# A head's normalised rows are transposed by DMAs in 16-bit planes instead of by TensorE

## The chip, the cores and the metric

The kernel runs on one core of one Trainium2 chip. The metric is the device time of one execution in microseconds (us). Before the change it is 894.45 us (median of 3 runs, 894.21 to 894.65). The engines that matter here are TensorE (PE in the profile, with PEld for its weight loads), VectorE (DVE), ScalarE (ACT), GpSimd (POOL) and SyncE (SP), which issues the DMAs.

## What is computed

One layer of a hybrid decoder: 16 learned meta tokens are put ahead of 2048 rows of 1024 features, the rows are normalised and multiplied by one input projection of eight groups of 512 columns, four groups feed a gated short convolution, four feed a retention layer of four heads, and the two results are joined, multiplied by an output projection, added to the input and normalised again. All is float32.

```
proj = rms_norm(h, norm_g) @ w_in                       # 2064 x 4096
cx, cb, cc, cg, q, k, v, rg = split(proj, 8)
conv_out = short_conv(cx, cb, cc) * silu(cg)
ret = head_group_norm(retention_chunkwise(rotary(q) * d**-0.5, rotary(k), v), ret_norm_g)
ret_out = ret * silu(rg)
y = rms_norm(h + concat(conv_out, ret_out) @ w_out, final_g)[16:]

def head_group_norm(o, g):                              # over the 128 features of a head
    y = (o - mean(o)) * rsqrt(var(o) + 1e-6)
    return y.reshape(rows, 512) * g
```

## The kernel before

The 2048 rows are taken in two blocks of 1024 (`r` = 0, 1), each as two halves of 512 rows (`j` = 0, 1). The projection is computed transposed: features lie on the 128 partitions and rows run along the free dimension, because a matmul there has a weight block as its stationary operand and 512 rows as its moving one. Each block runs through eight **units**: `UNITS` (line 37) gives their order. Units 0 to 3 are the heads of the retention, units 4 to 7 the groups of the convolution. After both blocks the output projection takes eight pairs of 128-row tiles.

A unit makes its projections in two **quads** (`quad`, line 203): seven products in the manner of Strassen and Winograd for a 2x2 arrangement of blocks, each product 12 matmuls of 128x512 (line 212), since every operand is split into a high and a low part and three of their four combinations are used. ACT casts the high part `wh` of a weight block (line 101), DVE subtracts it to get the low part `wl` (`sub`, line 113), from a ring of three buffers each, so that a cast waits until PE has finished the product three places back. Three of a quad's products are copied out of their PSUM bank by ACT (`copy`, line 219, tile `tc`, called here a bank copy), the second of them because PE then adds to the same bank. The results go to `take`, which adds, rotates or gates them on DVE and ACT.

A head (`head`, line 575) takes k and v from its first quad, q and the gate `sg` from its second. Then follow, for each half, transposes of k and v on PE (lines 631, 636), the state updates (646, 649), the scores (659, masked on DVE into the tile `pm`, line 661), the output `o` (669, 670), and the group norm: statistics on DVE (675, 677), a power on POOL (682), and four 128x128 operations on DVE that write the normalised rows `y` over `pm` (686). At that point rows lie on the partitions and features along the free dimension, while `sg` and all that follows has features on the partitions. So four PE matmuls against `ident` (line 693) transpose the four chunks of 128 rows into the PSUM tile `yT`, one DVE operation (694) multiplies `yT` by the norm's gain and by `sg`, and `store_mixed` (line 441, its DMA at 444) sends the half to DRAM in `mixed`, from which the output projection reads it. `pm` and `kd` (line 633) share two buffers (tag `b`), and so a head's `kd` waits until the `pm` of the head before is free.

The row tiles (`row_tile`, line 341) are 128x1024 float32 tiles in four buffers: the two rows of norm factors of each block, scratch at the start, loads for the output projection near the end, and `final_g`.

The program is recorded in this order, but its place on each engine is chosen by a scheduler, which moves an instruction ahead where its own timing says that another would wait; so the tail of a head stands among the matmuls of the next unit's quads. Each engine then runs its list in order, and SP too: a DMA that waits for its data holds up those behind it. Between heads SP also loads the raw weights of the following quads (`ra`, line 436) and eight tiles `x` or `w` (lines 361, 368), of which DVE makes sums that are stored for later (`prepare`, lines 181 to 191).

## Time and profile before

| | us |
|---|---|
| median of 3 runs | 894.45 |
| the profiled execution, its own time | 893.76 |
| the span of its instructions | 892.0 |
| of that, ACT busy | 407.2 |
| of that, POOL busy | 397.8 |

The profiled execution is 0.69 us below the median and just below the lowest run. The span begins with the first instruction and ends with the last, and 1.76 us of the execution's own time lie around it. The stretches of the span: the first block's units from about 57 to 365 us (heads to about 258, whose tail runs to 303), the second block's from 365 to 709 (heads to about 553, tails to 607), the output projection from 709 on.

How to read the rows: a timeline row has the start, the time from start to end, the engine, the line of the kernel, the operation, the tiles it writes and reads with their shape, a count, and in brackets how long the engine had been idle and who released it. PE's matmuls are pipelined: each overlaps the next, so the time from one start to the next is what a matmul takes of the engine, and its duration is longer. Each matmul of the lines 646, 659, 669 and 670, on plain float32 operands, appears as two records; those of line 212 and the transposes as one.

### The profile page before, as it was taken

What the parts mean: (1) busy time and instruction counts of PE and PEld (TensorE: products, weight loads), DVE (VectorE), ACT (ScalarE), POOL (GpSimd) and SP (SyncE); (2) the same over time, 40 slices, a digit from 0 to 9 for tenths busy, and PEclk for the clock granted to TensorE, in tenths of its full rate; (3) what the DMA queues carried; (4) which work ended last, traced back from release to release, by engine and by line L of the source; (5) the groups of instructions that cost most, each with busy time, mean ns of one, the idle gap of its engine ahead of it and who ended that gap; (6) DMA issues with size and microseconds to landing.
All of it is one profiled execution on the core that took longest, in us unless ns stands there. A gap on an engine that the chain in (4) does not pass through costs nothing.

```text
span 892.0 us, 12867 instructions
## 1 busy us (share of the span) xinstructions
PE 879.8 (99%) x4407; PEld 725.0 (81%) x4407; DVE 717.7 (80%) x1176; ACT 407.2 (46%) x816; POOL 397.8 (45%) x291
## 2 busy tenths in 40 slices
PE   8999999999999999999999999999999999999996
PEld 5778788888888778888888888888888888788885
DVE  6788887988967966999889899777668699766764
ACT  8674424234245364746243332423333476545553
POOL 0554222313134654452323323345546454787773
PEclk9999999999999999999999999999999999999999
DMA  9711224354224252834135272313131393555532
GB/s 336 231 65 48 72 54 150 129 159 149 73 83 142 83 154 75 293 117 141 48 95 200 71 245 87 96 58 95 49 93 49 117 390 101 183 165 160 183 121 81
DMA packets 76242, 116.94 MB, mean 131 GB/s; under 512 B 7632, under 2 KB 24336, under 8 KB 76176
## 3 DMA queue, kind: packets, MB, share of 16 engines
q1 hardware_dynamic: 76176, 116.11, 40.3%
q8 instruction: 35, 0.57, 0.3%
q14 instruction: 31, 0.25, 0.1%
HBM read 90.92 MB, written 25.17 MB: 130 GB/s over the span
## 4 chain that ended last, share of the span: by engine, by line
PE 82%; DVE 8%; DMA 4%; issue 2%; ACT 2%; POOL 2%; SPq 0%; POOLq 0%; DVEq 0%; ACTq 0%
PE pj L212 66%; PE pj L262 6%; DVE ml L113 2%; PE ms L669 1%; PE ms L670 1%; PE ms L659 1%; PE ms L646 1%; DMA w<-in_w_out 1%; DMA ra<-in_w_in 1%; PE ms L397 1%; DVE wl L113 1%; PE ms L693 1%; DVE ml L105 1%; PE ms L631 1%; PE ms L636 1%
## 5 line engine op out<-in xcount | busy, mean ns | idle before, releaser
L212 PE MATMUL pj<-mh,wl 128*128 128x512 f32 x1008 | 399.1, 396 | 1.5 <-ACT wh L101 0.6
L212 PE MATMUL pj<-ml,wh 128*128 128x512 f32 x1008 | 393.3, 390 | 0.0
L212 PE MATMUL pj<-mh,wh 128*128 128x512 f32 x1008 | 393.0, 390 | 0.0
L101 ACT CAST wh<-ra 128x512 fp32r<-128x512 f32 x216 | 134.0, 621 | 311.0 <-PE pj L212 264.9
L212 PEld LDWEIGHTS pj<-mh,wl 128*128 128x128 f32 x1008 | 189.4, 188 | 43.2 <-issue 2.2
L113 DVE TENSOR_TENSOR wl<-ra,wh 128x512 fp32r<-128x512 f32 x216 | 194.1, 899 | 34.5 <-ACT wh L101 34.0
L212 PEld LDWEIGHTS pj<-mh,wh 128*128 128x128 f32 x1008 | 189.2, 188 | 39.9
L212 PEld LDWEIGHTS pj<-ml,wh 128*128 128x128 f32 x1008 | 189.5, 188 | 37.8 <-issue 0.5
L113 POOL TENSOR_TENSOR ra<-ra 128x512 f32<-128x512 f32 x72 | 112.8, 1566 | 84.1 <-DVE qg L614 32.3
L110 POOL TENSOR_TENSOR sa<-ra 128x512 f32<-128x512 f32 x36 | 54.9, 1526 | 120.6 <-DVE wl L113 53.1
L113 POOL TENSOR_TENSOR ra<-sa,ra 128x512 f32<-128x512 f32 x36 | 52.0, 1444 | 92.6 <-DVE wl L113 89.1
L219 ACT COPY tc<-pj 128x512 f32<-128x512 f32 x108 | 62.7, 580 | 0.0
L262 PE MATMUL pj<-ml,mh 128*128 128x512 f32 x128 | 50.2, 392 | 0.1
L262 PE MATMUL pj<-mh,mh 128*128 128x512 f32 x128 | 49.9, 392 | 0.0
L262 PE MATMUL pj<-mh,ml 128*128 128x512 f32 x128 | 48.7, 397 | 0.7 <-DVE ml L113 0.6
L682 POOL TENSOR_TENSOR rp<-rs,neg_half 128x4 f32<-128x4 f32 x16 | 19.9, 1246 | 48.1 <-DVE rs L110 47.8
L723 DVE TENSOR_TENSOR yo<-pj,yo 128x512 f32<-128x512 f32 x32 | 21.9, 686 | 17.6 <-PE pj L212 7.8
L101 ACT CAST wh<-sa 128x512 fp32r<-128x512 f32 x36 | 22.4, 621 | 29.1 <-PE pj L212 28.9
L522 POOL TENSOR_TENSOR c<-c,rr 128x512 f32<-128x512 f32 x14 | 26.1, 1865 | 19.6 <-DVE c L459 9.6
L686 DVE TENSOR_SCALAR pm<-ms,mv,rp 128x128 f32<-128x128 f32 x64 | 21.9, 404 | 15.8 <-POOL rp L682 15.8
L522 POOL TENSOR_TENSOR c<-c,tc 128x512 f32<-128x512 f32 x14 | 26.1, 1862 | 18.7 <-ACT tc L548 18.7
L728 POOL TENSOR_TENSOR z<-yo,final_g 128x512 f32<-128x512 f32 x16 | 26.9, 1682 | 15.9 <-DVE yo L723 15.9
(137 smaller groups left out, 1145.5 us busy)
## 6 DMA issues: line engine op xcount, KB each, us to landing
ra<-in_w_in SPq DMA_DIRECT2D x128, 256.0 KB, 2.7
x<-in_xT SPq DMA_DIRECT2D x48, 256.0 KB, 4.8
w<-in_w_out SPq DMA_DIRECT2D x32, 256.0 KB, 5.2
ra<-mixed SPq DMA_DIRECT2D x32, 256.0 KB, 2.6
yo<-in_x SPq DMA_DIRECT2D x32, 256.0 KB, 4.5
ra<-in_x SPq DMA_DIRECT2D x16, 256.0 KB, 3.2
mixed<-c SPq DMA_DIRECT2D x16, 256.0 KB, 2.6
mixed<-qg SPq DMA_DIRECT2D x16, 256.0 KB, 2.3
```

Source lines behind the costliest of these rows:

```text
L101: nc.scalar.copy(out=hi, in_=src)
L105: nc.vector.scalar_tensor_tensor(out=lo, in0=src, scalar=scale, in1=hi.bitcast(F32), op0=ALU.mult, op1=ALU.subtract)
L110: eng.tensor_tensor(out=out, in0=a, in1=b, op=ALU.add)
L113: eng.tensor_tensor(out=out, in0=a, in1=b, op=ALU.subtract)
L212: nc.tensor.matmul(bank, a[:, ks], b, start=first and kt == 0 and n == 0, stop=kt == KH - 1 and n == 2, skip_group_check=not first,)
L219: nc.scalar.copy(out=c, in_=bank)
L262: nc.tensor.matmul(banks[i], a[:, ks], b, start=half + kt + n == 0, stop=half == 1 and kt == KH - 1 and n == 2,)
L522: eng.tensor_tensor(out=out, in0=a, in1=b, op=ALU.mult)
L682: nc.gpsimd.tensor_tensor(out=rp, in0=rs, in1=neg_half.rearrange("p (c a) -> p c a", a=1), op=ALU.pow)
L686: nc.vector.tensor_scalar(out=y[:, cs], in0=o[:, cs], scalar1=mv[:, c, 0:1], scalar2=rp[:, c, :], op0=ALU.subtract, op1=ALU.mult,)
L723: last[0] = nc.vector.tensor_tensor(out=y, in0=pp, in1=y, op=ALU.add)
L728: nc.gpsimd.tensor_tensor(out=ys[i][j], in0=y, in1=final_g[:, j * HB : (j + 1) * HB], op=ALU.mult)
```

## The change

PE's four transposes for each half, the PSUM tile `yT` and the DVE operation that read it go. In their place each half is transposed by one DMA:

- ACT copies `y` into a row tile `apart`, seen as 16-bit words: all low halves of the float32 words first, then all high halves (two planes of 512 words; line 716 after the change).
- SP issues a transposing DMA from `apart` to a second row tile `across`, eight blocks of 128x128 16-bit words (line 717).
- ACT puts the planes of `across` together again into float32 words, in `apart` (722). DVE multiplies by gain and gate as before, now from `apart` in SBUF (723), and `store_mixed` follows.

The first two steps (`turn`) are recorded within the next unit, after its first quad, and the last (`finish`) after its second quad. `catch_up` records them under `issue_after` the last bank copy of that quad, so that on ACT they stand behind the quad's bank copies. The two row tiles are those of the other block's pair (`rr0` or `rr1`, two buffers each instead of four in common), which hold nothing at that time.

```diff
     def quad(w, m, take):
         def copy(bank):
             c = sb.tile([P, HB], F32, name="tc", tag="tc", bufs=COPIES)
-            nc.scalar.copy(out=c, in_=bank)
+            copied[0] = nc.scalar.copy(out=c, in_=bank)
             return c
...
-    def row_tile(name):
-        return sb.tile([P, BLK], F32, name=name, tag="rr", bufs=4)
+    def row_tile(name, pair):
+        return sb.tile([P, BLK], F32, name=name, tag=f"rr{pair}", bufs=2)
...
+    def halves(a):
+        return a.bitcast(U16).rearrange("p (n two) -> p two n", two=2)
+
+    def planes(a):
+        return a.bitcast(U16).rearrange("p (two n) -> p two n", two=2)
+
+    waiting = [[], []]
+
+    def catch_up(stage):
+        if waiting[stage]:
+            with tc.issue_after(copied[0].ins):
+                while waiting[stage]:
+                    waiting[stage].pop(0)()
...
             quad(stationary(blocks[0]), m, take)
+            catch_up(0)
...
             quad(stationary(load_raw(w_loads(2 * h + 1))), m, take)
+            catch_up(1)
...
-            yT = ps_misc()
-            for c in range(CH):
-                cs = slice(c * P, (c + 1) * P)
-                nc.tensor.transpose(yT[:, cs], y[:, cs], ident)
-            nc.vector.scalar_tensor_tensor(
-                out=sg[j], in0=yT, scalar=ret_g[:, h : h + 1], in1=sg[j], op0=ALU.mult, op1=ALU.mult
-            )
-            store_mixed(r, j, KH + h, sg[j])
+            def turn(j=j, y=y, apart=turning[0][:, j * HB : (j + 1) * HB], across=turning[1][:, j * HB : (j + 1) * HB]):
+                nc.scalar.copy(out=planes(apart), in_=halves(y))
+                nc.sync.dma_start(
+                    across.bitcast(U16).rearrange("p (c f) -> p c f", c=2 * CH), apart.bitcast(U16), transpose=True
+                )
+
+                def finish():
+                    nc.scalar.copy(out=halves(apart), in_=planes(across))
+                    nc.vector.scalar_tensor_tensor(
+                        out=sg[j], in0=apart, scalar=ret_g[:, h : h + 1], in1=sg[j], op0=ALU.mult, op1=ALU.mult
+                    )
+                    store_mixed(r, j, KH + h, sg[j])
+
+                waiting[1].append(finish)
+
+            waiting[0].append(turn)
...
+                if turning is None:
+                    turning = [row_tile(name, 1 - r) for name in ("apart", "across")]
```

The convolution groups call `catch_up` in the same two places. Three places show how the lists of the engines move; all are of the first block, where the tail of head 1 runs beside the quads of head 2. Numbers behind a name tell one buffer from another and differ between the two programs.

On PE, in head 2's first quad before the change, the transposes of half 0 (line 693) stand with the scores of half 1 (659):

```order
L212 MATMUL pj_1935<-mh02_139,wl_1904 128x512
L212 MATMUL pj_1935<-ml02_140,wh_1903 128x512
L212 MATMUL pj_1935<-mh02_139,wh_1903 128x512
L693 MATMUL ms_1667<-ident_70,pm_1638 128x128
L659 MATMUL ms_1674<-qg_1512,kv_1358 128x128
L693 MATMUL ms_1667<-ident_70,pm_1638 128x128 x3
L659 MATMUL ms_1674<-qg_1512,kv_1358 128x128 x3
L212 MATMUL pj_1935<-mh03_145,wl_1904 128x512
```

After the change the scores of half 1 (now line 682) follow at once on the last output matmuls of half 0 (now lines 692 and 693, which were 669 and 670):

```order
L692 MATMUL ms_1638<-kv_1365,pm_1636 128x128
L693 MATMUL ms_1638<-state_1598,qg_1440 128x128
L682 MATMUL ms_1665<-qg_1504,kv_1346 128x128 x4
L215 MATMUL pj_1816<-mh50_234,wl_1760 128x512
L215 MATMUL pj_1816<-ml50_235,wh_1759 128x512
L215 MATMUL pj_1816<-mh50_234,wh_1759 128x512
```

The scores of half 1 move ahead by 33 of the 128x512 matmuls (before, 33 lie between the outputs of half 0 and the scores of half 1). The output of half 1 came 15 such matmuls behind its scores, and comes 24 behind them now.

On ACT, in head 2's second quad before the change, there are casts and bank copies (219), ahead of the gate (615):

```order
L585 COPY kv_1892<-pj_1783 128x512
L101 CAST wh_1915<-ra_1894 128x512
L101 CAST wh_1919<-sa_1902 128x512
L219 COPY tc_1948<-pj_1935 128x512
L101 CAST wh_1923<-ra_1898 128x512
L101 CAST wh_1927<-ra_1896 128x512
L219 COPY tc_1982<-pj_1935 128x512
L101 CAST wh_1931<-ra_1900 128x512
L219 COPY tc_1997<-pj_1984 128x512
L101 CAST wh_2266<-ra_2060 128x512
L615 ACTIVATE qg_2011<-qg_2011 128x512
```

The same stretch after the change, with one row more at its head:

```order
L716 COPY apart_729<-pm_1636 128x1024
L606 COPY kv_1876<-pj_1767 128x512
L102 CAST wh_1903<-ra_1882 128x512
L102 CAST wh_1907<-sa_1890 128x512
L222 COPY tc_1936<-pj_1923 128x512
L102 CAST wh_1911<-ra_1886 128x512
L716 COPY apart_729<-pm_1670 128x1024
L102 CAST wh_1915<-ra_1884 128x512
L222 COPY tc_1970<-pj_1923 128x512
L102 CAST wh_1919<-ra_1888 128x512
L222 COPY tc_1985<-pj_1972 128x512
L722 COPY apart_729<-across_730 128x2x512 x2
```

The copies into planes (716) come one ahead of the last `kv` copy and one among the second quad's casts, ahead of two of its three bank copies. Both copies back (722) come behind the third bank copy, ahead of the cast for the next unit's first product (101 before, 102 now) and of the gate.

On SP, at the same place before the change, the two stores of `mixed` (444) have weight loads between them, and the eight loads of `x` (361) stand behind the second store:

```order
L436 DMA ra<-in_w_in 128x512 x3
L444 DMA mixed_88<-qg 128x4x128
L436 DMA ra<-in_w_in 128x512 x2
L415 DMA mr<-in_rot_m 16x256
L436 DMA ra<-in_w_in 128x512
L444 DMA mixed_89<-qg 128x4x128
L361 DMA x<-in_xT 128x512 x8
```

After the change:

```order
L439 DMA ra<-in_w_in 128x512 x2
L717 DMA_TRANSPOSE across<-apart 128x8x128
L439 DMA ra<-in_w_in 128x512 x2
L717 DMA_TRANSPOSE across<-apart 128x8x128
L439 DMA ra<-in_w_in 128x512
L418 DMA mr<-in_rot_m 16x256
L439 DMA ra<-in_w_in 128x512
L447 DMA mixed_88<-qg 128x4x128
L447 DMA mixed_89<-qg 128x4x128
L364 DMA x<-in_xT 128x512 x8
```

A transposing DMA stands about where the first store stood and one among the weight loads behind it; both stores now stand together ahead of the `x` loads.

More of the change, by code (lines that the diff above doesn't have):

```diff
@@ L11 @@
 BF16 = mybir.dt.bfloat16
+U16 = mybir.dt.uint16
 AF = mybir.ActivationFunctionType
@@ L201, in prepared @@
                 parts(m, SUMS[n], kt, a)
+    copied = [None]
     def quad(w, m, take):
@@ L339, in spread_factors @@
         return rc2, ev
-    def row_tile(name):
-        return sb.tile([P, BLK], F32, name=name, tag="rr", bufs=4)
+    def row_tile(name, pair):
+        return sb.tile([P, BLK], F32, name=name, tag=f"rr{pair}", bufs=2)
     def row_factors(r, f):
-        f.extend([row_tile("rr"), row_tile("rr2"), []])
+        f.extend([row_tile("rr", r), row_tile("rr2", r), []])
         for j in range(2):
@@ L573, in rotary, with head @@
         turned[0] = nc.vector.tensor_tensor(out=a, in0=a, in1=rot[:, :w], op=ALU.add)
-    def head(h, r, m, rot_t, f, blocks, ahead, first=(), between=()):
+    def halves(a):
[8 more added lines that the diff above has]
+                    waiting[stage].pop(0)()
+    def head(h, r, m, rot_t, f, turning, blocks, ahead, first=(), between=()):
         between = iter(between)
@@ L597, in head @@
             quad(stationary(blocks[0]), m, take)
+            catch_up(0)
         next(between, lambda: None)()
@@ L621, in head @@
             quad(stationary(load_raw(w_loads(2 * h + 1))), m, take)
+            catch_up(1)
         next(between, lambda: None)()
@@ L805, in hybrid_trunk @@
             nc.sync.dma_start(cols, t["cols"])
-            t3 = [a[:, i * HB : (i + 1) * HB] for a in (row_tile("t3") for _ in range(2)) for i in range(2)]
+            t3 = [a[:, i * HB : (i + 1) * HB] for a in (row_tile("t3", 1) for _ in range(2)) for i in range(2)]
             t1 = [brief("t1") if n < BRIEF else sb.tile([P, HB], F32, name="t1", tag="tc", bufs=COPIES) for n in range(KH)]
@@ L835, in hybrid_trunk @@
         units = UNITS[r]
+        turning = None
         special = (first, between)
@@ L843, in hybrid_trunk @@
             elif unit < NG:
-                blocks = head(unit, r, m, rot_t, f, blocks, rest, *(special if unit == 0 else ()))
+                if turning is None:
+                    turning = [row_tile(name, 1 - r) for name in ("apart", "across")]
+                blocks = head(unit, r, m, rot_t, f, turning, blocks, rest, *(special if unit == 0 else ()))
                 if unit > 0:
@@ L850, in hybrid_trunk @@
                     idle = sb.tile([P, 2, BLK], F32, name="held", tag="rot_t", bufs=1)
-                    areas = [idle[:, 0], idle[:, 1], row_tile("held"), row_tile("held")]
+                    areas = [idle[:, 0], idle[:, 1], row_tile("held", 0), row_tile("held", 0)]
                     for i, a in enumerate(areas):
@@ L861, in hybrid_trunk @@
     m, b = moving(load_w_out)
-    final_g = row_tile("final_g")
+    final_g = row_tile("final_g", 1)
     nc.sync.dma_start(final_g, t["final_g"].partition_broadcast(P))
```

## The prediction

> **What bounds the kernel now.** I read the page's busy times first, then PE's waits, then busy time by stretch (each row: the stretch, its length, busy us of PE, PEld, DVE, ACT, POOL with record counts, granted clock, DMA share, GB/s).
>
> ```profile
> PE 879.8 (99%) x4407; PEld 725.0 (81%) x4407; DVE 717.7 (80%) x1176; ACT 407.2 (46%) x816; POOL 397.8 (45%) x291
> ...
> PE pj L212 <- ACT wh L101: 0.6, 1, 0.6
> ...
> PE ms L693 <- DVE pm L686: 0.3, 1, 0.3
> ...
> 107.00:303.00 196.00, 196.00 (x1126) 163.59 (x1125) 164.37 (x338) 74.90 (x163) 65.75 (x52) 1.00 0.36 115
> 414.00:553.00 139.00, 138.68 (x734) 118.19 (x734) 123.77 (x230) 47.29 (x92) 42.99 (x28) 1.00 0.39 124
> 553.00:709.00 156.00, 156.00 (x735) 130.59 (x734) 114.27 (x172) 56.11 (x100) 75.59 (x57) 1.00 0.25 75
> ```
>
> PE is the bound, at a granted clock of 1.00. Beside the heads' tails (first and second row) it is never idle for more than 0.3 us in all, and its longest waits there are tenths. DVE is next: 164 of 196 us and 124 of 139. So an instruction taken from PE shortens the span by its slot, as long as the others keep their distance.
>
> **What a transpose costs PE.** The group of all 64 transposes, and one group of four that stands alone among 128x512 matmuls, with eight score records of another head from the chain:
>
> ```profile
> L693 PE MATMUL ms<-ident,pm 128*128 128x128 f32 x64 | 12.2, 274 | 0.3 <-DVE pm L686 0.3
> ...
> 140.26 0.39 PE L212 MATMUL pj<-ml,wh 128*128 128x512 f32 x1
> 140.48 0.39 PE L212 MATMUL pj<-mh,wh 128*128 128x512 f32 x1
> 140.72 0.60 PE L693 MATMUL ms<-ident,pm 128*128 128x128 f32 x4
> 141.07 0.48 PE L212 MATMUL pj<-mh,wl 128*128 128x512 f32 x1
> 141.38 0.40 PE L212 MATMUL pj<-ml,wh 128*128 128x512 f32 x1
> ...
> 112.76 0.89 PE ms L659 x8
> ```
>
> The 274 ns of a record are latency; the slot is what counts. From 140.48 to 141.38 are 0.90 us, and two 128x512 matmuls take 2 x 0.227 of it, so four transposes cost 0.446 us, the switch back included. The chain's row agrees: eight small records in 0.89 us, 0.111 each. There are 8 heads x 2 halves = 16 such groups: 16 x 0.445 = **7.1 us**. The scores that stood with half of them stay, now merged with the output group.
>
> A rule of the Trainium skill weighs differently: "TensorE: Matmul & The Clock Gate", section "Part 4: PE-mode transpose", gives about 275 ns for a transpose in one kernel's context. The record's 274 ns agree with it, the 0.111 us slots do not; by 275 ns each, 64 would free 17.6 us.
>
> **The rest of the change, where it must hide.** ACT gets 16 copies into planes and 16 back, of 1024 words each. No ACT copy here is so long; nearest are these two groups and, from the second quad of head 2, the place where the copies will stand:
>
> ```profile
> L219 ACT COPY tc<-pj 128x512 f32<-128x512 f32 x108 | 62.7, 580 | 0.0
> ...
> L403 ACT COPY mk<-ms 16x128 f32<-16x128 f32 x32 | 8.1, 254 | 2.0 <-PE ms L397 1.6
> ...
> 185.89 0.62 ACT L101 CAST wh<-ra 128x512 fp32r<-128x512 f32 x1 [3.94 <-PE pj L212]
> 186.42 0.58 ACT L219 COPY tc<-pj 128x512 f32<-128x512 f32 x1
> 188.57 0.62 ACT L101 CAST wh<-ra 128x512 fp32r<-128x512 f32 x1 [1.57 <-PE pj L212]
> 189.10 0.58 ACT L219 COPY tc<-pj 128x512 f32<-128x512 f32 x1
> 191.29 0.62 ACT L101 CAST wh<-ra 128x512 fp32r<-128x512 f32 x1 [1.62 <-PE pj L212]
> ```
>
> 580 ns for 512 and 254 for 128 make 0.85 ns a word, so 1.02 us for 1024; if strides of two words cost double it is 2.0. I take 1.0: 32 us more on ACT, 407 to 440 of 892. ACT waits 1.6 to 3.9 us for PE between casts, which covers a copy; two in a row (line 722, 2.04 us) begin at 189.68 and push the cast of 191.29 to 191.7.
>
> When is the data there? The rows of half 1 set it, in the tail that runs beside head 2:
>
> ```profile
> 168.59 0.39 PE L670 MATMUL ms<-state,qg 128*128 128x128 f32 x2
> ...
> 181.13 0.38 PE L669 MATMUL ms<-kv,pm 128*128 128x128 f32 x2
> ...
> 188.54 1.37 DVE L686 TENSOR_SCALAR pm<-ms,mv,rp 128x128 f32<-128x128 f32 x4 [0.91 <-POOL rp L682]
> ...
> 191.96 0.74 DVE L694 SCALAR_TENSOR_TENSOR qg<-ms,ret_g,qg 128x512 f32<-128x512 f32 x1
> ...
> mixed<-qg SPq DMA_DIRECT2D x16, 256.0 KB, 2.3
> sums_w<-w SPq DMA_DIRECT2D x16, 256.0 KB, 2.0
> ...
> q1 hardware_dynamic: 76176, 116.11, 40.3%
> ```
>
> Half 0's output ends at 168.98. Now scores (0.89) and 24 matmuls (5.45) follow, so half 1's output starts at 175.3 instead of 181.13. `y` was whole at 189.91, 8.8 us after that start; with the same lag it is whole at 184.1. ACT, waiting for it since the cast at 181.33, copies until 185.1, ahead of the 185.89 cast.
>
> No transposing DMA is in the trace. Below, I bound issue to landing by the quickest transfer of its size, 2.0 us. Above: its output has pieces of 128 words of 16 bits, 1024 pieces, 64 for each of 16 engines; queue q1's packets take 0.403 x 892 x 16 / 76176 = 0.075 us on average, so 64 of them 4.8 us, and with 2.0 for the rest 6.8. I take 3, near the store of `mixed`, whose packets are the shortest of the large transfers. In a sentence by itself: the Trainium skill, "DMA: Bandwidth & Descriptors", section "Latency and other measured facts", has 261 GB/s for a DMA transpose, an estimate of 1.0 us for the 256 KB without the fixed part. So half 1 lands at 188, between 187.1 and 191.9; ACT comes to it at 189.7. On SP the transposes hold up weight loads behind them by at most these few us, and those serve products after 200.
>
> What is late next, if it slips? Behind ACT's copies back stand the cast of 191.29 and, through DVE and SP's second store, the `x` loads:
>
> ```profile
> 192.62 0.68 DVE L113 TENSOR_TENSOR wl<-ra,wh 128x512 fp32r<-128x512 f32 x1
> ...
> 204.22 0.68 DVE L113 TENSOR_TENSOR wl<-ra,wh 128x512 fp32r<-128x512 f32 x1
> ...
> 199.95 0.48 PE L212 MATMUL pj<-mh,wl 128*128 128x512 f32 x1
> ...
> 207.20 0.48 PE L212 MATMUL pj<-mh,wl 128*128 128x512 f32 x1
> ...
> 192.73 0.38 SPq L444 DMA_DIRECT2D mixed<-qg  x1
> 193.16 3.84 SPq L361 DMA_DIRECT2D x<-in_xT  x8
> ```
>
> The cast's low part is ready at 193.30 for a product at 199.95: 6.65 us of room. DVE's 723, of the 694's length, ends at 192.5 when the landing is in time, and the store goes out at about 192.7, as before. At the upper bound the copies back start at 191.9, and store and loads go out 2.0 us later; the sums of `x` then push the low part of 204.90, whose product starts at 207.20, and 2.3 us of room are there. Even the bound is covered, by 0.3 us. DVE's own work is the same in count and length (16 x 744 ns before, from PSUM).
>
> The second block is tighter. DVE at head 2's first quad there, and PE behind it:
>
> ```profile
> 489.16 0.65 DVE L113 TENSOR_TENSOR wl<-ra,wh 128x512 fp32r<-128x512 f32 x1
> ...
> 489.54 0.39 PE L212 MATMUL pj<-mh,wh 128*128 128x512 f32 x1
> 489.96 0.47 PE L212 MATMUL pj<-mh,wl 128*128 128x512 f32 x1
> ```
>
> PE waited 0.2 us here, since DVE had worked without a pause. In the new order DVE masks half 1's scores (0.74 us) ahead of this low part, but PE also gets half 1's output matmuls (about 1.7 us of slots) ahead of it, so I take nothing for the place, with bounds of -0.3 and +1.0 us for each of the three heads whose tail meets such a stretch.
>
> **The sum.** 892.0 - 7.1 = 884.9 us of span, with the 1.76 around it 886.7, against 893.76 for the profiled execution. That lies 0.69 below the median, so against the median the same sum is 894.45 - 7.1 = **887.4**. The bounds of the tight place move it from 886.5 to 890.4.
>
> **The rivals.** *Part given back* (0.13): ACT's in-order wait for `y`, or DVE's order in the second block, makes PE wait 0.5 us or more in most heads. For it: the 0.2 us wait above; against it: rooms of 2 to 6 us elsewhere. 2 to 4.5 us come back: 889.4 to 891.9. *Slower* (0.06): the transposing DMA lands later than assumed. From about 7.1 us to landing the 2.3 us of room at 207.20 are gone (half 1 leaves at 185.1, 189.7 is free, 192 is not), and each further us is one for PE in each of 8 heads. The gain is used up 0.9 us later, at 8.0; at 9 us it is 887.4 + 8 x 1.9 = 902.6. The trace's largest transfers of this size (5.2 us for `w`, on a loaded queue) speak against it, the missing row for it. *No effect* (0.07): DVE, at 84 to 89% beside the heads, becomes the bound, and PE waits for what it saves: 893 to 895. Against it: DVE still pauses for POOL and ACT there. *The whole record is freed* (0.02): PE's slots in the trace speak against it, but if a transpose blocked PE for its 274 ns, 17.5 us would go: 876.9. The page named above is on this side.
>
> **How the numbers follow.** The forecast has 0.70, and 0.02 is left for other gains. The range, 885.8 to 891.0, holds it and most of the first rival; below and above it lie less than two in ten. A difference of 0.2% (1.8 us) is about what a measurement of this kernel tells from none: faster means below 892.7. That is the forecast, the first and the last rival and the rest, 0.87; within it 0.07; slower 0.06.
>
> **What would show it.** Right: no PE record of 128x128 from `ident` and `pm`; PE idle by stretch still under 1 us beside the heads; landings of `across` at 2 to 5 us; the copies 716 and 722 at about 1.0 us; low parts of weights ahead of their products by 1 us or more. Wrong: PE waiting for ACT's casts or bank copies beside 716 and 722, landings over 7 us, copies over 2 us, or `x` and `w` loads that go out later against PE than before.

## The result, and the profile after

The changed kernel takes 886.98 us at the median (885.97 to 887.5, 4 runs), the kernel before 894.33 us beside it (893.01 to 894.65, 4 runs). The ratio is 0.9919, with an interval from 0.9902 to 0.9936. Forecast were 887.4 us, and 884.9 us of span.

The page of the changed kernel, its first line and the busy time of each engine:

```profile
span 884.9 us, 12802 instructions
...
PE 872.3 (99%) x4343; PEld 717.7 (81%) x4343; DVE 718.4 (81%) x1176; ACT 441.1 (50%) x848; POOL 400.4 (45%) x291
```

The span is 7.1 us shorter, PE's busy time 7.5 us (879.8 before). ACT has 34 us more, DVE is unchanged. What PE waits for in the changed kernel (us in all, times, longest):

```profile
PE ms L799 <- ACT warm L793: 2.3, 1, 2.3
PE pj L215 <- ACT tc L222: 1.0, 2, 0.6
PE pj L215 <- DVE wl L114: 0.7, 2, 0.4
PE ms L692 <- DVE pm L684: 0.4, 1, 0.4
```

The 2.3 us lie at the start of the program, and the kernel before has them too. The other waits are still tenths, and PE is as full as before beside the heads. Busy time of the changed kernel by stretch (columns as in the prediction):

```profile
107.00:303.00 196.00, 195.21 (x1108) 162.53 (x1107) 166.80 (x344) 93.27 (x181) 66.93 (x54) 1.00 0.43 128
414.00:553.00 139.00, 138.92 (x725) 118.12 (x724) 126.39 (x239) 58.29 (x105) 47.69 (x30) 1.00 0.42 125
```

PE idles 0.79 us in the first row and 0.08 in the second. ACT has 93.3 us in place of 74.9 and 58.3 in place of 47.3: that is where the copies went.

The place of the prediction, head 2's second quad: ACT's timeline of the changed kernel (start, duration, in brackets the idle time before the row and what ended it), then SP's:

```profile
182.72 1.05 ACT L716 COPY apart<-pm 128x1024 uint16<-128x1024 uint16 x1 [0.64 <-DVE pm L709]
...
186.94 0.62 ACT L102 CAST wh<-ra 128x512 fp32r<-128x512 f32 x1 [1.58 <-issue]
187.47 0.58 ACT L222 COPY tc<-pj 128x512 f32<-128x512 f32 x1
187.95 2.56 ACT L722 COPY apart<-across 128x1024 uint16<-128x1024 uint16 x2
190.36 0.61 ACT L102 CAST wh<-ra 128x512 fp32r<-128x512 f32 x1
```

```profile
184.33 1.24 SPq L717 DMA_TRANSPOSE across<-apart  x1
...
192.84 0.50 SPq L364 DMA_DIRECT2D x<-in_xT  x1
```

The copies back come right behind the bank copy, with no idle time before them, so the data was there; none of the 16 copies back has idle time before it. The weight cast behind them stands at 190.36. The loads of `x` begin at 192.84 (193.16 before). PE is further ahead by then: the product that started at 199.95 before starts at 197.60, so against PE these loads go out 2.0 us later. All 16 turns, from the view of the tile `across` (min, median and max; then first and last start):

```profile
L717 SPq DMA_TRANSPOSE across<-apart x16: 1232/1237/1358, 124.3 to 584.3; - x16
L722 ACT COPY apart<-across x16: 1345/1351/1367, 138.8 to 600.6; 128x1024 uint16<-128x1024 uint16 x16
...
DMA to landing us min/median/max: 2.7/3.1/5.4
```

Where the 7.1 us came from is read off the starts of the same matmul in both traces: the first one of the 15th, the 99th and the 197th of the 252 products of `quad` (lines 212 and 215). Before they start at 98.89, 403.16 and 709.57 us, in the changed kernel here:

```profile
98.92 0.48 PE L215 MATMUL pj<-mh,wl 128*128 128x512 f32 x1
...
399.01 0.39 PE L215 MATMUL pj<-mh,wl 128*128 128x512 f32 x1
...
701.54 0.39 PE L215 MATMUL pj<-mh,wl 128*128 128x512 f32 x1
```

So the first block's heads (99 to 403) gained 300.09 - 304.27 = -4.18 us, the second block's (403 to 710) -3.88, and the output stage behind them gave 0.92 back. The same for the experiments, from the same starts in one trace of each, in us against the kernel before:

```
                    to 99   99-403  403-710  710-end   span
the change           0.03    -4.18    -3.88     0.92   -7.12
e1_no_turn           0.56    -4.91    -0.23     0.74   -3.83
e5_no_turn_late      0.24    -3.19    -0.03     0.55   -2.43
e9_held_product      1.14    -5.28    -0.91     0.58   -4.47
e2_late_pe           0.31    -0.51     1.83    -0.03    1.60
e6_late_pe2          0.49    -0.73     0.76     0.14    0.66
e3_at_once           0.19    -0.83     5.91     0.52    5.78
e4_three_turns       0.54    -0.11    -3.15     1.03   -1.69
e7_double_copies     0.47    -3.39    -1.79     0.93   -3.80
e10_plain_dma        1.22    -4.21    -3.93     0.95   -5.97
e11_v_turn2          0.28     0.66    -4.11     0.81   -2.37
e12_pool_product     0.59    -2.64    -4.01     0.65   -5.42
e8_v_turn            1.13     8.59     7.85     0.08   17.64
```

The first column is ahead of every edit: up to 1.2 us of a single trace are scatter there. With 8 groups of four transposes in each block, the slots alone would give -3.56 in each of the two middle columns.

### The profile page after: what moved, and what is told of

Its sections match the earlier page's. It is cut to its first block, busy times and chain, and to the rows that moved or that the text cites. A ratio compares the mean times of both kernels' runs of the same rounds, so it can differ in the third digit from the quotient of the medians.

```text
span 884.9 us, 12802 instructions
## 1 busy us (share of the span) xinstructions
PE 872.3 (99%) x4343; PEld 717.7 (81%) x4343; DVE 718.4 (81%) x1176; ACT 441.1 (50%) x848; POOL 400.4 (45%) x291
## 2 busy tenths in 40 slices
DMA packets 93137, 121.12 MB, mean 137 GB/s; under 512 B 24528, under 2 KB 41232, under 8 KB 93072
## 3 DMA queue, kind: packets, MB, share of 16 engines
q1 hardware_dynamic: 93072, 120.31, 43.0%
## 4 chain that ended last, share of the span: by engine, by line
PE 56%; DVE 6%; DMA 2%; issue 2%; ACT 1%; POOL 1%; SPq 0%; POOLq 0%; DVEq 0%; ACTq 0%
PE pj L215 50%; DVE ml L114 2%; PE pj L265 2%; DVE wl L114 1%; PE ms L682 1%; PE ms L669 1%; DVE ml L106 1%; PE ms L693 1%; PE ms L692 1%; DMA t<-sums_w 1%; DMA n<-in_x 1%; POOL yo L111 0%; DMA yo<-in_x 0%; DMA ra<-in_w_in 0%; DVE pm L709 0%
## 5 line engine op out<-in xcount | busy, mean ns | idle before, releaser
L758 ACT ACTIVATE rot<-yo 128x512 f32<-128x512 f32 x32 | 20.2, 630 | 26.8 <-DVE yo L756 25.8
```

The lines of the kernel that those rows point to most:

```text
L758: nc.scalar.activation(junk, y, AF.Square, accum_out=ss[:, i, j : j + 1])
```

## The experiments

### What taking the transposes off PE is worth by itself

**e1_no_turn.** The kernel before without its transposes:

```diff
-            yT = ps_misc()
-            for c in range(CH):
-                cs = slice(c * P, (c + 1) * P)
-                nc.tensor.transpose(yT[:, cs], y[:, cs], ident)
             nc.vector.scalar_tensor_tensor(
-                out=sg[j], in0=yT, ...
+                out=sg[j], in0=y, ...
```

> The kernel before, with the 64 transposes on PE left out and nothing in their place: VectorE's last product reads y as it stands, so the attention rows come out untransposed (this part of the computation is left out). No copies into planes, no transposing DMA, the order of before. Theory (slots): 16 groups x 0.445 us = 7.1 us, 887.2 us, span about 884.9. Rival (the whole 274 ns record is freed): 876.8. Rival (the 7.1 us of the change come from its new order, and taking the transposes out in the old order leaves PE waiting for VectorE): 891 or more.

Measured: 890.05 us, before 894.65; ratio 0.9951 (0.9939 to 0.9963). Only 4.6 us are gained, less than by the change, which does more work. None of the three theories gave this number; the third came nearest. The table shows where: the first block has its slots (-4.91), the second gains nothing (-0.23). PE's waits of this kernel, and DVE's timeline beside the first quad of head 1 of the second block:

```profile
PE pj L212 <- ACT tc L219: 2.3, 2, 1.2
...
PE pj L212 <- DVE kv L110: 1.8, 3, 0.7
```

```profile
437.18 1.36 DVE L686 TENSOR_SCALAR pm<-ms,mv,rp 128x128 f32<-128x128 f32 x4 [0.91 <-POOL rp L682]
438.58 0.75 DVE L690 SCALAR_TENSOR_TENSOR qg<-pm,ret_g,qg 128x512 f32<-128x512 f32 x1
...
439.86 0.88 DVE L675 BATCH_NORM_STATS2 st<-ms 128x6 f32<-128x128 f32 x4
...
442.33 1.36 DVE L686 TENSOR_SCALAR pm<-ms,mv,rp 128x128 f32<-128x128 f32 x4 [1.12 <-POOL rp L682]
443.62 0.68 DVE L110 TENSOR_TENSOR kv<-pj,tc 128x512 f32<-128x512 f32 x1
```

And the PE row behind it:

```profile
444.35 0.50 PE L212 MATMUL pj<-mh,wl 128*128 128x512 f32 x1 [0.73 <-DVE kv L110]
```

The last product (line 690 here, 0.75 us) is ready as soon as the rows of half 0 are normalised, and DVE takes it at 438.58, ahead of the statistics of half 1. Those, POOL's power, the normalised rows and the sum of `kv` behind them in DVE's order all come that much later. The sum of `kv` reads a PSUM bank, and the next product on PE waits for the bank: 0.73 us here, and so at three heads. The gaps between PE's starts in this stretch that exceed a slot are 1.00, 0.80 and 0.79 us there and 1.51 at 599.99 (0.11 of each of the first three, and 0.23 of the last, are the slot): 3.5 us. Without them the second block would have -3.8, its slots. So the slots were freed, and 2.2 us of them went to the three waits for the sum of `kv`. The other 1.3 us, at 599.99, are a wait for a bank copy, which stands in ACT's order behind a silu that waits 4.2 us for DVE, in the first convolution group behind the heads.

**e5_no_turn_late.** The order of the change, with nothing of the turn in it:

```diff
             def turn(...):
-                nc.scalar.copy(out=planes(apart), in_=halves(y))
-                nc.sync.dma_start(...)
                 def finish():
-                    nc.scalar.copy(out=halves(apart), in_=planes(across))
                     nc.vector.scalar_tensor_tensor(
-                        out=sg[j], in0=apart, ...
+                        out=sg[j], in0=y, ...
```

> The changed kernel with the whole turn left out: no copies into planes, no transposing DMA, no copies back; the last product reads y untransposed (this part of the computation is left out) at the change's late place, behind the second quad's last bank copy. The order of the change alone, without PE's transposes and without the DMA path. Theory (the DMA path is wholly hidden, and the late place of the last product is what the kernel without transposes in the old order, 890.1 us, lacked): 886 to 887.5, as the change. Rival (copies and DMAs of the change cost PE something): 884 to 885.5. Rival (the order is worth nothing, and the 2.9 us between the first experiment and the change come from elsewhere): 889.5 to 890.5.

Measured: 890.63 us, before 893.99; ratio 0.9966 (0.9953 to 0.9978): next to the second rival. This too is slower than the change, although it does nothing that the change doesn't. The second block again gains nothing (-0.03), with the same three waits and the one behind the heads, 3.8 us in all; in the first, PE waits 1.8 us for the mask of head 2's scores at 217.11. DVE's timeline at the same place shows that recording the product late didn't make it late on DVE:

```profile
440.09 0.75 DVE L718 SCALAR_TENSOR_TENSOR qg<-pm,ret_g,qg 128x512 f32<-128x512 f32 x1
440.76 0.69 DVE L114 TENSOR_TENSOR wl<-ra,wh 128x512 fp32r<-128x512 f32 x1
```

**e9_held_product.** The same kernel, with the product held back by data:

```diff
                 def finish():
+                    late = small.tile([P, 1], F32, name="late", tag="late")
+                    nc.vector.scalar_tensor_tensor(
+                        out=late, in0=copied[1][:, 0:1], scalar=0.0, in1=ret_g[:, h : h + 1], op0=ALU.mult, op1=ALU.add
+                    )
                     nc.vector.scalar_tensor_tensor(
-                        out=sg[j], in0=y, scalar=ret_g[:, h : h + 1], ...
+                        out=sg[j], in0=y, scalar=late, ...
```

Here `copied[1]` is the tile of the second quad's last bank copy.

> The fifth experiment's kernel (no transposes, no copies, no DMA; y is read untransposed, so this part of the computation is left out) with the last product held back by data: its per-partition factor is made on VectorE by a product of one column from the second quad's last bank copy (times 0, plus ret_g), so that it cannot start before that copy. Theory (in the fifth experiment the ready product slipped into VectorE's chain from statistics to normalised rows, 0.75 us that made PE wait for the sums of kv; in the change the DMA path holds it back): the three waits of 0.7 to 1.0 us beside heads of the second block go, and with them most of the wait of 1.95 us at 215: 885 to 887. Rival (the product's place is worth nothing): 890 to 891.

Measured: 889.13 us, before 894.82; ratio 0.9939 (0.9927 to 0.9952). The time missed both theories, 2 us above the first. The mechanism it was to show is there. The same place on DVE, and PE's largest wait:

```profile
437.39 1.37 DVE L710 TENSOR_SCALAR pm<-ms,mv,rp 128x128 f32<-128x128 f32 x4 [0.91 <-POOL rp L706]
438.67 0.68 DVE L114 TENSOR_TENSOR wl<-ra,wh 128x512 fp32r<-128x512 f32 x1
```

```profile
PE pj L215 <- ACT tc L222: 3.6, 3, 1.5
```

The product no longer stands between, PE's waits for the sum of `kv` are gone, and the first block has -5.28. What remains are waits for ACT's bank copies, which stand behind a silu that waits for DVE: gaps of 1.88 us at 597.94 and 1.29 at 675.89 (0.23 of each is the slot). Without these 2.7 us the second block would have -3.6, its slots; with them it gains only 0.7 us on the first experiment. The second of them lies in a convolution group that no edit touches. There a low part on DVE runs beside a product on POOL that began 0.5 us before it, in this kernel and then in the change:

```profile
669.58 1.73 POOL L526 TENSOR_TENSOR c<-c,rr 128x512 f32<-128x512 f32 x1 [1.45 <-DVE c L463]
...
670.08 1.78 DVE L114 TENSOR_TENSOR wl<-sa,wh 128x512 fp32r<-128x512 f32 x1
```

```profile
667.70 2.34 POOL L525 TENSOR_TENSOR c<-c,rr 128x512 f32<-128x512 f32 x1 [1.36 <-DVE c L462]
...
668.21 0.68 DVE L114 TENSOR_TENSOR wl<-sa,wh 128x512 fp32r<-128x512 f32 x1
```

DVE's operation takes 1.1 us longer here and POOL's 0.6 us less, and the wait on PE beyond its slot is 1.1 us. Ahead of the wait at 597.94 the same low part takes 1.79 us, and 1.78 in the four other experiments without the turn, which all wait at that place (e1, e5, and e2 and e6 below). It takes 0.68 in the change, e4, e7, e10, e11 and e12, which do not wait there. It is not the only condition: in the kernel before it takes 1.77 and PE does not wait, in e3 0.68 and PE does. What decides which of the two operations becomes the longer one is not shown.

**e2_late_pe and e6_late_pe2.** The order of the change with the transposes on PE. In the second experiment `turn` does them:

```diff
-                nc.scalar.copy(out=planes(apart), in_=halves(y))
-                nc.sync.dma_start(...)
+                yT = ps_misc()
+                for c in range(CH):
+                    nc.tensor.transpose(yT[:, c * P : (c + 1) * P], y[:, c * P : (c + 1) * P], ident)
+                nc.scalar.copy(out=apart, in_=yT)
                 def finish():
-                    nc.scalar.copy(out=halves(apart), in_=planes(across))
```

> The changed kernel with the turn put back on PE at its new place: after the first quad's last bank copy come four transposes into PSUM and one ScalarE copy of 512 words into the idle row tile; the last product and the store come after the second quad's last bank copy as in the change. The order of the change without its DMA and its plane copies. Theory (slots): PE takes the 7.1 us back, 894 us, and 893 if the two waits of 0.74 and 0.44 us that vanished in the change stay away. Rival (the new order, not the PE slots, brings the gain): 887 to 889.

Measured: 896.61 us, before 894.65; ratio 1.0022 (1.0011 to 1.0032), 2.6 us above its theory. ACT's new copy waits in its order for PE's transposes, 9.1 us in all. PE's largest wait is for bank copies:

```profile
PE pj L215 <- ACT tc L222: 3.3, 3, 2.1
```

The longest, 2.1 us at 607.71, is the one behind the silu of the first convolution group, which waits 5.2 us for DVE, and not one behind the new copy. So what the 2.6 us are is not shown.

In the sixth, `finish` does them, into PSUM for the last product, without the copy:

```diff
                 def finish():
-                    nc.scalar.copy(out=halves(apart), in_=planes(across))
+                    yT = ps_misc()
+                    for c in range(CH):
+                        nc.tensor.transpose(yT[:, c * P : (c + 1) * P], y[:, c * P : (c + 1) * P], ident)
                     nc.vector.scalar_tensor_tensor(
-                        out=sg[j], in0=apart, ...
+                        out=sg[j], in0=yT, ...
```

> The changed kernel with four PE transposes into PSUM at the late place itself, right ahead of the last product, which reads PSUM as before; no ScalarE copy, no DMA. The order of the change with its PE slots given back, without the ScalarE copy that stood in its way in the second experiment. Theory (slots add to the order): 887.0 + 7.1 = 894.1. Rival (PE transposes at that place hold ScalarE and VectorE up as in the second experiment): 895.5 to 897.

Measured: 894.85 us, before 893.99; ratio 1.0008 (0.9999 to 1.0017), near the first theory. The late order by itself is worth nothing, or costs up to a us and a half. So neither the order nor the missing transposes alone make the change's 7.1 us. Beside the slots it takes something that keeps the last product out of DVE's chain: e9 shows that for the three waits at the heads, and in the change it is the turn's own way, through two copies and a DMA. The change is also without the waits behind the silu of the convolution, 1.3 to 2.7 us in the experiments without the turn; what keeps them away there was not tested, and e9, which still has them, cannot be told from the change by its interval alone (0.9927 to 0.9952 against 0.9902 to 0.9936).

### What the way through ACT and the DMA costs

**e3_at_once.** The copies back right behind the copies into planes:

```diff
-                waiting[1].append(finish)
+                waiting[0].append(finish)
```

> The changed kernel with the copies back, the products and the stores right behind both copies into planes, at the first quad's last bank copy, so that ScalarE waits in its order for the landing of half 1 (3.1 us) and then copies back 2.7 us before its next cast. Theory (rooms): casts come 5.3 us later than in the change, their products have 4.8 to 5 us of room there, so PE waits 0.5 to 1 us in each of 8 heads: 891 to 895. Rival (the place of the copies back does not matter, ScalarE is half idle): 886.5 to 888. Rival (the whole wait reaches PE): 8 x 5.3 us more, 929.

Measured: 897.24 us, before 894.65; ratio 1.0035 (1.0021 to 1.0048). The loss against the change is 10 us, 2 us more than the first theory's upper end. ACT and PE of this kernel, at head 2's second quad, and the group of the copies back (busy, mean ns, idle before):

```profile
189.26 1.33 ACT L722 COPY apart<-across 128x1024 uint16<-128x1024 uint16 x1 [3.66 <-DMA across<-apart]
...
190.98 0.58 ACT L222 COPY tc<-pj 128x512 f32<-128x512 f32 x1
```

```profile
191.61 0.50 PE L215 MATMUL pj<-mh,wl 128*128 128x512 f32 x1 [1.85 <-ACT tc L222]
```

```profile
L722 ACT COPY apart<-across 128x1024 uint16<-128x1024 uint16 x16 | 21.7, 1358 | 32.4 <-DMA across<-apart 32.4
```

ACT stands 32.4 us in all for landings. Here PE waits for a bank copy (222): I had reckoned with the casts' rooms of 4.8 us, and the bank copies behind the same instruction have less. In the second block PE waits for low parts of weights too, 2.4 us at three heads, and the longest wait, 3.2 us at 608.46, is again for a bank copy behind the silu of the convolution. A landing of 3 us that ACT waits for in its order costs more than the whole gain.

**e4_three_turns.** Three transposing DMAs one after the other:

```diff
-                nc.sync.dma_start(across..., apart..., transpose=True)
+                for a, b in ((apart, across), (across, apart), (apart, across)):
+                    nc.sync.dma_start(b..., a..., transpose=True)
```

> The changed kernel with three transposing DMAs for each half, one after the other (across from apart, apart from across, across from apart again; the rows come out the same), so that the data lands about 9.3 us after the copy into planes instead of 3.1. The second and third wait on SP for the one before. Prediction's price (1 us for each us beyond 7.1 us of landing, in each of 8 heads): 887 + 8 x 2.2 = 905. Rival (the rooms are wider than the price says, since ScalarE comes to the copies back 4 us after the copies into planes and casts have 4 to 6 us more): 887 to 890.

Measured: 892.38 us, before 894.65; ratio 0.9971 (0.996 to 0.9981): 5.1 us above the change (-2.3 us against its own before, where the change has -7.4). Neither theory had it. SP and ACT at the same place, and one PE row:

```profile
185.32 1.24 SPq L718 DMA_TRANSPOSE across<-apart  x1
...
188.74 1.24 SPq L718 DMA_TRANSPOSE apart<-across  x1
...
191.63 1.24 SPq L718 DMA_TRANSPOSE across<-apart  x1
...
197.42 0.50 SPq L364 DMA_DIRECT2D x<-in_xT  x1
```

```profile
183.70 1.05 ACT L716 COPY apart<-pm 128x1024 uint16<-128x1024 uint16 x1 [0.59 <-DVE pm L709]
...
194.81 1.36 ACT L723 COPY apart<-across 128x1024 uint16<-128x1024 uint16 x1 [3.54 <-DMA across<-apart]
```

```profile
192.05 0.35 DVE L423 TENSOR_TENSOR mk<-mk,mr 16x64 f32<-16x64 f32 x2 [2.73 <-DMA mr<-in_rot_m]
```

```profile
218.74 0.49 PE L692 MATMUL ms<-kv,pm 128*128 128x128 f32 x2 [2.04 <-DVE pm L684]
```

Half 1 is back 10.1 us after its copy into planes (184.75 to 194.81; in the change it is about 3.9: issue at 184.33 and 3.4 to its own landing, behind a copy that ended at 183.77). ACT stands 12.6 us in all for landings, against 32.4 in e3. Two loads that stand behind the turns on SP go out later than in the change: those of `x` by 4.6 us, and the small one of `mr` (line 418, the rotary table of the meta tokens) by 3.0 (190.04 against 187.04). For `mr` DVE stands idle 2.7 us, 1.3 in the change. DVE's work behind both comes later, with it the mask of head 2's scores, and PE waits 2.0 us for that ahead of 218.74. The prediction named only the loads of `x`. By the fifth experiment they are not needed for such a wait: there they go out at 189.88, earlier than in the change, and PE still waits 1.8 us for the same mask, behind another late landing of `mr`:

```profile
191.59 0.35 DVE L423 TENSOR_TENSOR mk<-mk,mr 16x64 f32<-16x64 f32 x2 [2.14 <-DMA mr<-in_rot_m]
```

What each of the two loads costs in e4 was not separated. In the second block, where neither is loaded, the delay costs 0.7 us in all (-3.15 against -3.88).

**e7_double_copies.** Each ACT copy done twice:

```diff
+                nc.scalar.copy(out=planes(apart), in_=halves(y))
                 nc.scalar.copy(out=planes(apart), in_=halves(y))
...
+                    nc.scalar.copy(out=halves(apart), in_=planes(across))
                     nc.scalar.copy(out=halves(apart), in_=planes(across))
```

> The changed kernel with each copy into planes and each copy back done twice (32 more ScalarE copies, 16 x 1.05 + 16 x 1.35 = 38 us more on ScalarE; the rows come out the same). Theory (ScalarE's pauses cover them): the four copies back push one cast by 2.7 us, of rooms of 4.8 to 5 us, so 886.5 to 888.5. Rival (ScalarE's order is as tight as the third experiment's loss of 10 us for 5.3 us of delay suggests): 5 us more, 892.

Measured: 889.33 us, before 893.99; ratio 0.9947 (0.9934 to 0.9961): 2.7 us above the change, between the two theories. PE's longest wait for a bank copy is 1.7 us now (0.6 in the change):

```profile
PE pj L215 <- ACT tc L222: 2.5, 2, 1.7
```

ACT's pauses cover the copies that the change has, but not as many again: its order matters although it is busy half of the time. PE also waits 1.5 us for masks of scores (0.4 in the change); where these come from was not traced.

**e10_plain_dma.** A plain DMA of the same size in the transposing one's place:

```diff
-                    across.bitcast(U16).rearrange("p (c f) -> p c f", c=2 * CH), apart.bitcast(U16), transpose=True
+                    across.bitcast(U16), apart.bitcast(U16)
```

> The changed kernel with a plain DMA of the same 256 KB from apart to across in place of the transposing one (the rows come out untransposed; this part of the computation is left out). Theory (rooms): the landing shortens from 3.1 to 2.0 to 2.5 us, and nothing waits for it, so 886.5 to 887.5. Rival (the small pieces of the transposing DMA hold back other transfers, weight loads and x loads): 884 to 886.

Measured: 887.47 us, before 894.82; ratio 0.9919 (0.9906 to 0.9933), the change's own ratio, as the first theory had it. Its tile `across`:

```profile
L717 SPq DMA_DIRECT2D across<-apart x16: 465/471/520, 125.5 to 585.4; - x16
...
DMA to landing us min/median/max: 2.2/2.4/4.3
```

The transposing form lands 0.7 us later (3.1 against 2.4) and holds SP 0.77 us longer (1.24 against 0.47); nothing here waits for either.

### Attempts at a faster kernel

**e8_v_turn and e11_v_turn2.** The same turn for `v`, whose 64 transposes (line 659) are still on PE. In the eighth, GpSimd multiplies `v` by the row factors, and the copy into planes stands in the second quad:

```diff
+        tv = [[gen("tv")[:, :HB] for _ in range(2)] for j in range(2)]
+        for j in (1, 0):
+            nc.gpsimd.tensor_tensor(out=v[j], in0=v[j], in1=f[1][:, j * HB : (j + 1) * HB], op=ALU.mult)
...
+                nc.scalar.copy(out=planes(a), in_=halves(v[j]))
+                nc.sync.dma_start(b..., a..., transpose=True)
...
-                nc.tensor.transpose(tp[:, c * P : (c + 1) * P], v[j][:, c * P : (c + 1) * P], ident)
...
-                nc.scalar.mul(vj[:, cs], tp[:, cs], f[2][j][0][:, c : c + 1])
+            nc.scalar.copy(out=halves(vj), in_=planes(tv[j][1]))
```

> The changed kernel with v's 64 transposes taken off PE in the same way: GpSimd multiplies v by the row factors squared ahead of its turn (so the four ScalarE scalings of each half fall away), ScalarE copies it into planes behind the second quad's first bank copy, a transposing DMA turns it into two further tiles of k and v's ring, and the copy back stands where the scalings stood. Theory (slots): 16 groups of four transposes, 0.41 to 0.445 us each, 6.6 to 7.1 us off 887.0: 880. Rival (two more ScalarE copies beside the first ones, and GpSimd's products ahead of its powers, make PE wait half to one us in each head): 883 to 887. Rival (v comes back later than the state update needs it): 890 or more.

Measured: 913.29 us, before 893.99; ratio 1.0217 (1.02 to 1.0233), the last rival. PE's largest wait, 13.7 us in 8 places, is for bank copies, and ACT itself waits for the landing of `v` in 10 of its 16 copies back. In the eleventh, the copies into planes and the DMAs stand right behind the first quad, the copy back and the scalings behind the scaling of `k`, and GpSimd has no part:

```diff
+        for j in (1, 0):
+            a, b = tv[j]
+            nc.scalar.copy(out=planes(a), in_=halves(v[j]))
+            nc.sync.dma_start(b..., a..., transpose=True)
         q, sg = [None, None], [None, None]
...
-            nc.scalar.mul(kd, tp, kd_col[:, h : h + 1])
+            scaled = nc.scalar.mul(kd, tp, kd_col[:, h : h + 1])
...
+            with tc.issue_after(scaled.ins):
+                nc.scalar.copy(out=halves(flat), in_=planes(tv[j][1]))
+                for c in range(CH):
+                    cs = slice(c * P, (c + 1) * P)
+                    nc.scalar.mul(vj[:, cs], flat[:, cs], f[2][j][0][:, c : c + 1])
```

> The changed kernel with v's 64 transposes taken off PE again, but with the turn some 15 us before it is needed: ScalarE copies v into planes right behind the first quad, the transposing DMAs follow at once, the copy back (1.35 us) and the four scalings stand behind the scaling of k. No GpSimd work is added. Theory (what cost 26 us in the eighth experiment was waiting for the landing and GpSimd's products ahead of its powers; with both gone PE's 6.6 to 7.1 us remain, less the 2.4 us that 38 us more on ScalarE cost in the seventh): 882 to 884. Rival (ScalarE's copies beside the heads are too many, its order makes PE wait at bank copies): 888 to 895.

Measured: 892.23 us, before 894.82; ratio 0.9974 (0.9963 to 0.9986), in the rival's range. The second block is no faster than in the change (-4.11 against -3.88), the first loses what it had gained (0.66). PE's two largest waits:

```profile
PE pj L215 <- DVE qg L111: 5.6, 3, 2.5
PE pj L215 <- ACT tc L222: 2.7, 6, 0.9
```

The rival's way, the bank copies, is the smaller of the two; the larger, for DVE's sums of `q`, was in neither theory.

**e12_pool_product.** The last product on GpSimd:

```diff
                 nc.scalar.activation(d, d, AF.Silu)
+                nc.scalar.mul(d, d, ret_g[:, h : h + 1])
...
-                    nc.vector.scalar_tensor_tensor(out=sg[j], in0=apart, scalar=ret_g[:, h : h + 1], in1=sg[j], ...)
+                    nc.gpsimd.tensor_tensor(out=sg[j], in0=apart, in1=sg[j], op=ALU.mult)
```

> The changed kernel with the last product taken off VectorE: ScalarE multiplies the gate by ret_g right behind its silu (16 more ScalarE operations of about 0.63 us, 10 us), and GpSimd multiplies it by the turned rows (16 products of about 1.5 us in place of VectorE's 16 x 0.74 us). It is possible since the turned rows now lie in SBUF, and is an attempt at a version faster than both. Theory (PE's slots are the bound after the change, its waits beside the heads add up to about 1.1 us): 886 to 887.5, no better than the change. Rival (VectorE, 84 to 91% busy beside the heads, still costs PE something): 884 to 885.5. Rival (GpSimd's products lengthen VectorE's operations beside them, 0.68 to 1.77 us in these traces, and delay the powers): 888 to 892.

Measured: 887.97 us, before 893.87; ratio 0.9932 (0.9918 to 0.9946), half a us above the first theory and no better than the change, whose interval it overlaps. Taking 12 us off DVE doesn't make it faster: PE's wait for the mask of head 2's scores, 0.4 us in the change, is 0.9 here. No version here beats the change.

## Why the prediction was right, point by point

- **The slots, 7.1 us.** Right in size, and rather small. Take each wait on PE of more than 0.2 us beyond a slot out of the two middle columns: the change then comes to -4.6 and -3.7, e1 to -4.4 and -3.3, e5 to -4.2 and -3.4 and e9 to -4.3 and -3.2, where 3.56 was worked out for each, and e6, with its transposes on PE, to 0.2 and -0.2. That makes 7.5 to 8.2 us of slots. The other size, 275 ns for a transpose by the Trainium skill, "TensorE: Matmul & The Clock Gate", section "Part 4: PE-mode transpose", would have freed 17.6 us, an estimate from that figure; no run with the transposes off PE gained more than 7.4.
- **When half 1 is there.** `y` was forecast whole at 184.1, and ACT takes it at 182.72. The landing was taken as 3 us, and is 3.1 at the median (2.7 to 5.4). ACT was forecast at the copies back at 189.7, and comes at 187.95 without idle time. The upper bound took 1024 pieces for each DMA and their time as 4.8 us; queue q1 has 16896 packets more than before (93072 against 76176), 1056 for each, and all of the time to landing is 3.1 us.
- **ACT's copies.** Into planes 1.05 us, with 1.0 forecast. Back 1.35, a third above the 1.0: the one duration that was mis-sized. It cost nothing that shows, because ACT's pauses for PE still covered it, but the seventh experiment shows that the cover is not wide.
- **The second block's tight place, taken as nothing.** Right in number, and for a reason that was only half given. DVE and PE of the changed kernel there:

```profile
485.19 0.66 DVE L114 TENSOR_TENSOR wl<-ra,wh 128x512 fp32r<-128x512 f32 x1
```

```profile
487.84 0.39 PE L215 MATMUL pj<-mh,wl 128*128 128x512 f32 x1
```

  The low part is done 2.0 us ahead of its product, where PE had waited 0.2. But the sum assumed that the freed slots shorten the span "as long as the others keep their distance", and by e1 and e5 they don't by themselves: DVE's chain then makes PE wait at three heads and once behind them, 3.5 us in e1. The prediction looked for DVE's delay at the low part and the mask. It didn't see that the turn's latency also holds the last product back, which is worth 2.2 us of waits at three heads. The other 1.3 us of e1 lie behind the heads. The sum took nothing there, and nothing came, but no run shows why; as far as is known that part is luck.
- **The rival "No effect".** It was refused for the whole kernel, rightly. For the second block alone it is what e1 and e5 measured (-0.23 and -0.03).
- **The rival "Slower" by a late landing.** The way it names, through loads that stand behind the turn on SP, shows in e4, but with two corrections: the small load of `mr`, which the prediction left out, is on it too, and PE waits for the mask of head 2's scores, not for the low part named with 207.20. Its price failed too: "each further us is one for PE in each of 8 heads". At 10.1 us that is 8 x 3.0 = 24 us above the change, and 5.1 were measured, so 8.0 us is not the point where the gain is used up. The step that failed is the 8: the way exists only beside heads of the first block, where `x` and `mr` are loaded. It was a rival and no part of the sum.
- **Signs of being wrong that came.** Two did, and cost tenths. Against PE the loads of `x` go out 2.0 us later than before, and PE waits 0.43 us for the mask of head 2's scores at 215.50. And PE waits 0.36 us for a bank copy at 287.94, beside the tail of head 3.
- **What cancelled.** The sum has no term for 0.9 us given back in the output stage, nor for as much gained elsewhere. The waits do not explain that gain: before, PE stood 0.74 us too long at 305.29 and 0.44 at 509.34, beyond a slot, and no longer does, but the waits at 215.50 and 287.94 are new, 0.59 and 0.52 beyond a slot. What is left for it are slots somewhat larger than 0.445 us for a group. In the output stage PE's waits of over 0.2 us beyond a slot grow from 0.5 to 1.3 us. A cast there waits for a load that it didn't wait for before, which may be behind it; that was not traced:

```profile
724.81 0.62 ACT L102 CAST mh<-t 128x512 fp32r<-128x512 f32 x1 [0.60 <-DMA t<-sums_w]
```

  All kernels here with these transposes off PE give 0.5 to 1.0 us back in that stage, but for e8 (0.08), and the two with them on PE -0.03 and 0.14. That the spans agree to 0.1 us is therefore partly luck; that they agree to a us is not.

## What to carry to other kernels

Taking an instruction off the engine that bounds frees its slot only if the work that it held back stays out of the way: an operation that becomes ready early is taken early, and on the next busiest engine it can stand ahead of something that the first engine needs. So ask of a removed step what it delayed, and hold that back by data where the order doesn't. Held back by data alone, the product of e9 freed PE of three waits, and others came elsewhere. A detour of several us through another engine and a DMA costs nothing where the result is waited for late, and the whole gain where an engine with other work waits for it in its order. Look also at the small loads that stand behind a new DMA in its queue: an engine may be waiting for one of them.

## What the hardware showed that was not expected

- A transposing DMA of 256 KB from SBUF to SBUF in 16-bit elements holds its queue on SP 1.24 us and lands after 3.1 us; a plain one of the same size takes 0.47 and 2.4. The Trainium skill, "Advanced Engine Details and Errata", section "X-Bar Transpose (TRN2)", says that transposing DMAs are as fast as regular ones on this chip; these rows do not agree, by 0.7 us to landing.
- An ACT copy of 1024 16-bit words that reads every second word and writes them in a row takes 1.05 us; the reverse, in a row to every second word, takes 1.35.
- The low parts `wl` and the products of `tc` with `rr` are DVE operations on 128x512 float32 elements. In the changed kernel the 151 of them that ran while POOL did nothing took 0.66 to 0.69 us; the 115 that overlapped a POOL operation took 0.67 to 1.79, and 64 of these more than 1 us.
